# Other places in the planned order of two attentions: longer listed tasks of TensorE and other numbers for the kinds of tasks

## The chip, the cores and the metric

The kernel runs on one core of a Trainium2 chip, as one program. The metric is the device time of one execution in microseconds (us). A core has five engines that run side by side and wait for one another by semaphores: TensorE (PE, matrix products; its weight loads are shown as PEld), VectorE (DVE), ScalarE (ACT), GpSimd (POOL), and SyncE (SP), which here issues the transfers (DMAs). Each engine takes its instructions in the order in which the program lists them. PE writes its results to PSUM, eight banks of 512 fp32 columns on 128 partitions; the other data lie in SBUF.

## The reference

A decoder trunk of two layers on 1024 tokens of width 1024, with 16 heads of 64, all in fp32. What matters here are the two token mixers; each is followed by a gated MLP with a causal convolution.

```python
# layer 0: forgetting attention, per block of 128 queries
s = einsum('bhqd,bhkd->bhqk', qb, k) * scale
s = s + cb[..., :, None] - c[..., None, :]        # c: cumulated log of the forget gates
s = where(kpos <= qpos, s, -inf)
o = einsum('bhqk,bhkd->bqhd', softmax(s), v)
h = h + o @ w_out
...
# layer 1: sparse attention, two groups of 8 heads that share keys and values
p_c = softmax over 63 compressed keys;  o_c = p_c @ vc
o_s = softmax(q k_sel) @ v_sel   # 16 of 16 blocks of 64 tokens are chosen: causal attention
o_w = softmax(q k_win) @ v_win   # a window of 512 tokens
o = g0 * o_c + g1 * o_s + g2 * o_w
h = h + o @ w_out
```

## The kernel before, in words

An fp32 product is made from three matmuls: an operand is split into a high part (the value rounded to fp32r) and a low part (the rest), and high x high, high x low and low x high are added up in PSUM (lines 216 to 218, `mm3`). So most results pass ACT, which writes the high part, and then DVE or POOL, which writes the low part.

The stages follow each other: projections of the first attention; the forgetting attention; the rest of its output projection; the first MLP; projections of the second attention; the sparse attention; the second MLP.

**The planner.** In both attentions the order of instructions on each engine isn't written by hand: `Flow` (lines 103 to 175) holds a list of tasks, each with an engine, an estimated duration, a place and the buffers that it takes and gives back, and plays them through in time when the program is made. At each step it looks, on each engine, for the tasks that can start earliest, takes the one with the smallest place among them, and emits its instructions. The chip then runs each engine's list in that order. A task's place is `u` plus the number of its kind in `PLAN`; `gap` is added to the listed duration of PE's tasks alone:

```python
t = Task(eng, dur + (self.plan.get("gap", 0) if eng == "PE" else 0), u + self.plan.get(kind, 0), ...)
...
first = min(at for at, _ in c)
at, _, t = min(((at, t.prio, t) for at, t in c if at <= first), key=lambda x: x[1])
```

**Kinds in both attentions**, for a block of four times 128 queries of one head (first attention) or of 128 queries and four heads (second):
- R: PE makes scores into one of two score rooms of two PSUM banks (`scores`, line 585; the mask by line 590). M: DVE takes the maximum (lines 594, 599). E: ACT takes the exponential and its sum (line 602). D: DVE takes the reciprocal (line 605). N: POOL scales the probabilities (line 606).
- K, at u + 1 + x, with x from 0 to `spread` over the key blocks: PE turns up to four blocks of 128 x 128 into one of three banks `t` (line 619). H: ACT writes the high part (line 630). L: DVE the low part (line 632), into one of five or four buffers. V: PE adds the value product into the bank `v`, of which there is one (lines 624 and 625; a step is K, H, L, V in turn).
- J: ACT and DVE take the finished sum out of the bank `v` and join its halves (lines 644 and 648). O: in the sparse attention, POOL splits the joined rows.
- F and G: the first and the other seven steps of a half row of the output projection on PE, into a bank `t` (`proj_tasks`, line 835; F also turns rows for the next stage's norm). W: ACT and POOL split projection weights (`split_tasks`, lines 865 and 866). Q: everything else, all transfers on SP among it.

**The forgetting attention** (`fox_attn`, line 745). u counts 32 blocks: the first 24 are, for each of heads 0 to 7, its first and second half of queries and the first half of head h + 8; the last eight are the second halves of heads 8 to 15. A block in the first half has 4 blocks of keys, one in the second half 8. Beside them the planner lists the **late projections** (`late_tasks`, line 660): values, queries and keys of heads 8 to 15 for the second half of the tokens, 12 rows of eight steps (P is the first step of a row, S the others and the turn), row n at place `late` + 1.6 n with `late` = 2. A step is three matmuls of 512 columns, listed as .665 us plus `gap`. A row holds one of the three banks `t`. Rows of queries and keys then pass a norm of each head (`heads`, line 696: lines 708, 704, 249, 241, 242, 245 to 248, 707) and are stored to HBM (line 727), from where heads 8 to 15 load them (line 765). Loads of a head go out on SP in the order of u. The output projection of five row tiles can start when all 24 first blocks are joined. Probabilities have two buffers for each row of a block.

**The sparse attention** (`nsa_attn`, line 1960). Tiles of 128 queries go from the last to the first, i = 7 to 0, so with 1024 down to 128 keys. Each has two groups; a group has the compressed keys first (`cmp_tasks`, u grows by .5) and then four blocks (two quads of heads, each with all keys and with the window; u grows by 1 each). A tile's output projection (F, G) follows its joins. At the start three late rows of queries are projected (P) and normed (L246 to L248, L1519), and the output weights are split after them (W, place 2 + 3 k).

Of the kernel before, what the change touches and what calls it, by code (L numbers as in the profile page):

```python
# [16 lines left out]
P = 128  # L17
T = 1024
D = 1024
NT = T // P  # L20
ND = D // P
H = 16
HD = 64
G = 2
# [26 lines left out]
def moved(*shape):  # L51
# [2 lines left out]


PLAN = {
    "fox": dict(F=1e3, G=-11.5, R=.5, M=5, E=-1, K=-.5, H=-1.5, L=-5.5, V=2, J=-4, D=1.5, N=18.5, Q=1.5, W=13, P=-3, S=0, O=1, spread=.7, wo=.6, wo_from=21, side=2, late=2, step=1.6, gap=.015),
    "ffn0": {"": 18.5, "A": -1.5, "B": -11, "C": -11, "D": -10, "I": 4.5, "P": -12, "R": 14.5, "S": -6, "T": 23, "U": 24, "V": 23, "W": -7, "a": -2.5, "b": -12, "c": 12, "d": -7, "e": -12, "f": -4, "g": -20, "h": -8, "l": 21, "n": 16.5, "r": -8, "s": -6, "t": -6, "x": 23.5, "y": 23.5},
    "ffn1": {"": 0, "A": 12.5, "B": -4, "C": -12, "D": 12.5, "I": 15.5, "P": -11.5, "R": 3.5, "S": 12, "T": 18, "U": 24, "V": 17, "W": 4.5, "a": -12, "b": 8, "c": -12, "d": -3, "f": 0.5, "l": 19.5, "n": -11, "s": 17.5, "t": -8},
    "nin": {"": 0},  # L60
    "nsa": dict(P=5.5, S=-6, F=18, G=1e3, R=-6.5, M=11.5, E=.5, D=-5.5, K=-6, H=1, L=-2.5, V=9.5, J=13.5, O=24, N=0, Q=10, W=13, spread=.3, wo=3, wo_from=2, side=2, cmp=.5, gap=.02),
}


# [2256 lines left out]
```

## Time and profile before

| | |
|---|---|
| median of 3 runs | 2687.89 us (2687.56 to 2690.54) |
| the profiled execution: its own time | 2689.46 us |
| its span, first to last instruction | 2687.7 us |
| mean granted TensorE clock | 0.996 of full speed |
| forgetting attention | some 255 to 620 us of the span |
| sparse attention | some 1483 to 2045 us |

Times within the trace are us from the start of the span. Busy time of an engine is the union of its instructions; a matmul's end is modelled, since matmuls overlap, so that the start-to-start distance is the measure of its cost. Idle time before an instruction is shown in brackets with the releaser, the instruction that ended the last wait.

### The profile page before, as it was taken

How to read it: one execution, taken by the hardware profiler on the slowest of the kernel's cores; microseconds unless marked ns; L12 is line 12 of the kernel's file. 1: busy time of each engine (PE TensorE's matmuls, PEld its weight loads, DVE VectorE, ACT ScalarE, POOL GpSimd, SP SyncE). 2: the span in 40 equal slices, each digit the busy share in tenths (PEclk: the TensorE clock that was granted, in tenths of full speed). 3: DMA queues.
4: the chain of work that ended last, by engine and by line, in shares of the span. 5: the costliest groups of instructions: out<-in, count | busy, mean ns of one | idle time of the engine just before them, and what ended most of it. 6: DMA issues, size and time to landing. Idle time of an engine off the chain costs nothing.

```text
span 2687.7 us, 39265 instructions
## 1 busy us (share of the span) xinstructions
PE 2623.3 (98%) x13384; PEld 2178.8 (81%) x13384; DVE 2153.0 (80%) x4015; ACT 1509.1 (56%) x3168; POOL 550.4 (20%) x843
## 2 busy tenths in 40 slices
PE   8999999999999999999999999999999999999999
PEld 6778887787888888888898788888887788888887
DVE  6752778766987877889887888888987988777988
ACT  5331767655554545444674687777876555554443
POOL 1110444420000000000354564444452000000000
PEclk9999999999999999999999999999999999999999
DMA  6475666724422222734234310001123422224553
GB/s 183 107 170 174 178 164 179 203 64 152 127 87 94 71 94 86 272 120 157 100 97 123 94 60 13 33 29 36 41 68 120 136 96 77 93 72 168 188 173 129
DMA packets 276776, 310.84 MB, mean 116 GB/s; under 512 B 19944, under 2 KB 194448, under 8 KB 276576
## 3 DMA queue, kind: packets, MB, share of 16 engines
q1 hardware_dynamic: 276144, 306.76, 37.2%
q8 instruction: 106, 1.74, 0.3%
q10 hardware_dynamic: 432, 1.57, 0.2%
q14 instruction: 94, 0.77, 0.1%
HBM read 236.84 MB, written 71.43 MB: 115 GB/s over the span
## 4 chain that ended last, share of the span: by engine, by line
PE 63%; DVE 8%; ACT 2%; issue 1%; DMA 1%; POOL 0%; SPq 0%; DVEq 0%; ACTq 0%; POOLq 0%
PE ps L217 15%; PE ps L218 15%; PE ps L216 15%; PE t L619 4%; PE v L624 2%; PE s L1992 2%; PE v L625 2%; PE s L1991 2%; DVE op L1069 1%; PE t L216 1%; DVE sum L1069 1%; PE t L218 1%; PE t L217 1%; PE s L590 1%; DVE b L1069 1%
## 5 line engine op out<-in xcount | busy, mean ns | idle before, releaser
L1073 ACT CAST op<-sum 128x512 fp32r<-128x512 f32 x396 | 239.3, 621 | 401.5 <-PE ps L218 278.1
L216 PE MATMUL ps<-xs,op 128*128 128x512 f32 x880 | 342.6, 389 | 1.8 <-DVE u L1069 1.8
L217 PE MATMUL ps<-xs,op 128*128 128x512 f32 x880 | 342.5, 389 | 0.7 <-DVE xs L1069 0.7
L218 PE MATMUL ps<-xs,op 128*128 128x512 f32 x880 | 342.4, 389 | 0.0
L1069 DVE TENSOR_TENSOR op<-sum,op 128x512 fp32r<-128x512 f32 x396 | 266.9, 689 | 83.5 <-ACT op L1073 83.2
L602 ACT ACTIVATE pt<-s,sm 128x640 f32<-128x640 f32 (+7 forms) x384 | 275.0, 721 | 74.9 <-DVE sm L599 32.9
L632 DVE TENSOR_TENSOR p_l<-t,p_h 128x512 fp32r<-128x512 f32 x456 | 277.0, 628 | 47.5 <-ACT p_h L630 43.9
L630 ACT CAST p_h<-t 128x512 fp32r<-128x512 f32 x456 | 238.3, 545 | 112.9 <-PE t L619 109.4
L619 PE MATMUL t<-ident,pt 128*128 128x128 f32 x1632 | 242.7, 276 | 14.0 <-DVE p_l L632 6.9
L217 PE MATMUL ps<-op 128*128 128x512 f32 x616 | 239.9, 389 | 1.8 <-DVE op L1069 1.8
L216 PE MATMUL ps<-op 128*128 128x512 f32 x616 | 240.2, 390 | 0.4 <-ACT op L1073 0.4
L218 PE MATMUL ps<-op 128*128 128x512 f32 x616 | 239.7, 389 | 0.0
L606 POOL TENSOR_SCALAR pt<-pt,sm,gate 128x640 f32<-128x640 f32 (+7 forms) x256 | 199.3, 784 | 163.3 <-DVE sm L605 141.3
L599 DVE TENSOR_REDUCE sm<-s 128x1 f32<-128x640 f32 (+7 forms) x256 | 210.6, 833 | 24.9 <-PE s L590 20.4
L619 PEld LDWEIGHTS t<-ident,pt 128*128 128x128 f32 x1632 | 192.2, 142 | 46.8 <-DVE p_l L632 7.8
L1282 DVE SCALAR_TENSOR_TENSOR acc<-u,cw,acc 128x1023 f32<-128x1023 f32 (+1 forms) x176 | 225.7, 1283 | 4.1 <-ACT acc L1283 1.3
L216 PEld LDWEIGHTS ps<-xs,op 128*128 128x128 f32 x880 | 165.2, 188 | 37.2 <-issue 2.0
L217 PEld LDWEIGHTS ps<-xs,op 128*128 128x128 f32 x880 | 165.2, 188 | 35.1 <-DVE xs L1069 1.0
L218 PEld LDWEIGHTS ps<-xs,op 128*128 128x128 f32 x880 | 165.2, 188 | 34.3
L624 PE MATMUL v<-p_h,v 128*128 128x512 f32 (+1 forms) x376 | 157.9, 421 | 4.8 <-DVE o_early L648 2.5
L1073 ACT CAST op<-w_raw 128x512 fp32r<-128x512 f32 x132 | 81.5, 626 | 109.2 <-PE ps L218 103.9
L2216 POOL TENSOR_SCALAR h<-h,nt_rs 128x1024 f32<-128x1024 f32 x8 | 10.4, 1299 | 631.1 <-DVE nt_rs L248 612.4
(503 smaller groups left out, 6505.0 us busy)
## 6 DMA issues: line engine op xcount, KB each, us to landing
w_raw<-in_f_w_up SPq DMA_DIRECT2D x96, 512.0 KB
u<-in_f_w_down SPq DMA_DIRECT2D x176, 256.0 KB
s_g<-acc SPq DMA_DIRECT2D x40, 512.0 KB
g<-s_g SPq DMA_DIRECT2D x20, 1024.0 KB
w_raw<-in_a_w_in SPq DMA_DIRECT2D x32, 512.0 KB
qa<-s_q SPq DMA_DIRECT2D x32, 256.0 KB
ka<-s_k SPq DMA_DIRECT2D x32, 256.0 KB
v<-s_v SPq DMA_DIRECT2D x16, 512.0 KB
```

Of the source, the lines that this page charges most:

```text
L216: mm(out, a[0], b[0], start=start, stop=False, **kw)
L217: mm(out, a[0], b[1], start=False, stop=False, **kw)
L218: mm(out, a[1], b[0], start=False, stop=stop, **kw)
L599: b = a if joint else F.add("DVE", .066 + 1.0417e-3 * n, u, "M", lambda z=z, c=c: nc.vector.tensor_reduce(sm["nm"][:, c], src(ps.t, z), ax ...
L602: e = F.add("ACT", .238 + .8333e-3 * n, u, "E", lambda z=z, c=c, out=out: nc.scalar.activation(out(), src(ps.t, z), AF.Exp, bias=sm["nm"][ ...
L619: nc.tensor.transpose(t.t[:, r * P:(r + 1) * P], b(), self.ident)
L624: nc.tensor.matmul(out, v(), p2.t[0][:, :n], start=first, stop=False)
L630: h = F.add("ACT", .052 + .8333e-3 * n, u + 1 + x, "H", lambda: nc.scalar.copy(p2.t[0][:, :n], t.t[:, :n]), after=[a], uses=[t, p2])
L632: lambda: nc.vector.tensor_tensor(p2.t[1][:, :n], t.t[:, :n], f32(p2.t[0][:, :n]), op=OP.subtract), after=[h], uses=[t, p2])
L1069: TT = lambda out, a, b, op: nc.vector.tensor_tensor(out, a, b, op=op)
L1073: a = F.add("ACT", .53, u, "A", lambda: nc.scalar.copy(op.t[:, 0], src()), after, [op], uses)
L1282: return lambda: nc.vector.scalar_tensor_tensor(acc.t[:, sh:], o.t[:, :T - sh], cw[j][:, c:c + 1], acc.t[:, sh:], op0=OP.mult, op1=OP.add)
```

## The change

Only numbers of two plans change; the other plans, tasks, buffers and instructions are as before. The listed PE tasks are longer by .035 us (forgetting attention) and .03 us (sparse attention), and the kinds have other numbers.

```diff
-    "fox": dict(F=1e3, G=-11.5, R=.5, M=5, E=-1, K=-.5, H=-1.5, L=-5.5, V=2, J=-4, D=1.5, N=18.5, Q=1.5, W=13, P=-3, S=0, O=1, spread=.7, wo=.6, wo_from=21, side=2, late=2, step=1.6, gap=.015),
+    "fox": dict(F=1000.0, G=-8, R=-1.5, M=9.5, E=1.0, K=-2.0, H=-0.5, L=-12, V=0.5, J=0.5, D=9.5, N=22.5, Q=-11.0, W=3.5, P=-1.0, S=1.0, O=1, spread=0.7, wo=0.6, wo_from=21, side=2, late=2, step=1.6, gap=0.05),
...
-    "nsa": dict(P=5.5, S=-6, F=18, G=1e3, R=-6.5, M=11.5, E=.5, D=-5.5, K=-6, H=1, L=-2.5, V=9.5, J=13.5, O=24, N=0, Q=10, W=13, spread=.3, wo=3, wo_from=2, side=2, cmp=.5, gap=.02),
+    "nsa": dict(P=20.5, S=5.0, F=23.5, G=1000.0, R=4.5, M=12.0, E=20.0, D=-12, K=1.5, H=12.0, L=-10.0, V=20.0, J=14.0, O=22, N=19.0, Q=9.5, W=16.0, spread=0.3, wo=3, wo_from=2, side=2, cmp=0.5, gap=0.05),
```

## Rows read from the trace of the kernel before

**Rows 1.** The page's first part: each engine's busy time (share of the span) and its instructions.

```profile
PE 2623.3 (98%) x13384; PEld 2178.8 (81%) x13384; DVE 2153.0 (80%) x4015; ACT 1509.1 (56%) x3168; POOL 550.4 (20%) x843
```

**Rows 2.** Busy time by stage: the stretch in us from the span's start (the forgetting attention, then the sparse one), its length, each engine's busy us and instructions, the granted TensorE clock (1.00 is full), the DMA engines' busy share and GB/s.

```profile
255.00:620.00 365.00, 350.45 (x2029) 290.44 (x2028) 262.27 (x565) 238.54 (x560) 135.53 (x160) 0.99 0.57 161
...
1483.00:2045.00 562.00, 548.11 (x3520) 462.38 (x3520) 478.10 (x1016) 405.25 (x979) 279.69 (x378) 1.00 0.15 50
```

**Rows 3.** The same view, the forgetting attention cut finer; columns as in rows 2.

```profile
360.00:380.00 20.00, 18.01 (x111) 14.96 (x110) 17.10 (x42) 14.31 (x38) 5.86 (x8) 1.00 0.82 200
380.00:440.00 60.00, 59.48 (x354) 49.42 (x354) 47.53 (x115) 41.42 (x106) 24.36 (x32) 1.00 0.58 158
440.00:496.00 56.00, 46.17 (x270) 37.99 (x269) 43.39 (x95) 44.66 (x107) 37.44 (x40) 0.91 0.82 229
496.00:620.00 124.00, 123.75 (x693) 103.14 (x692) 80.58 (x141) 68.40 (x137) 26.84 (x27) 1.00 0.42 121
```

**Rows 4.** Two of these cuts with the instructions of line 217 alone, the second of each three matmuls of a projection step (up to 496 only late steps run it; columns: stretch, length, PE and weight loads, clock, DMA).

```profile
380.00:440.00 60.00, 12.55 (x32) 6.07 (x32) 1.00 0.58 158
440.00:496.00 56.00, 0.00 (x0) 0.00 (x0) 0.91 0.82 229
```

**Rows 5.** PE's waits from 436 to 496: who waited for whom, us in total, times, longest us.

```profile
PE t L619 <- DVE p_l L632: 4.0, 2, 2.2
PE v L624 <- DVE o_early L648: 2.5, 2, 1.5
PE v L624 <- DVE o_late L648: 2.0, 3, 0.8
```

**Rows 6.** Busy time in two short stretches between 440 and 496; columns as in rows 2.

```profile
448.80:455.60 6.80, 6.25 (x27) 5.97 (x28) 4.55 (x13) 4.49 (x11) 3.98 (x6) 0.50 0.85 261
...
486.30:489.70 3.40, 3.40 (x11) 2.69 (x12) 2.84 (x6) 2.40 (x7) 2.88 (x3) 0.50 0.81 255
```

**Rows 7.** Busy time in the sparse attention; columns as in rows 2.

```profile
1483.00:1530.00 47.00, 43.61 (x246) 34.06 (x246) 38.88 (x73) 29.39 (x60) 26.96 (x42) 0.96 0.33 92
...
1600.00:1900.00 300.00, 299.83 (x1946) 255.95 (x1945) 260.79 (x514) 216.79 (x485) 136.23 (x166) 1.00 0.08 26
1900.00:1960.00 60.00, 55.29 (x369) 45.96 (x367) 54.78 (x142) 48.83 (x143) 30.46 (x49) 1.00 0.18 62
```

**Rows 8.** PE in order of time (start us, us, instruction, xcount of like ones in a row): the first mask product of the blocks with u = 20 and with u = 25, which closes their first scores.

```profile
441.67 0.29 PE L590 MATMUL s<-mask_d,identb 128*128 128x128 bf16 x2
...
491.03 0.23 PE L590 MATMUL s<-mask_d,identb 128*128 128x128 bf16 x1
```

**Rows 9.** The timeline of all engines near 375, with the idle time before an instruction and what ended it: DVE's short operations of a late head's norm chain, POOL beside them, and PE.

```profile
374.85 0.17 DVE L246 TENSOR_TENSOR rs_t<-rs_t,rs_v 128x8 f32<-128x8 f32 x1
...
375.05 0.59 DVE L247 TENSOR_SCALAR rs_t<-rs_t 128x8 f32<-128x8 f32 x1
...
375.58 2.48 POOL L866 TENSOR_TENSOR w_l<-w_raw,w_h 128x512 fp32r<-128x512 f32 x2
375.67 1.19 DVE L248 TENSOR_TENSOR rs_r<-rs_y,rs_t 128x8 f32<-128x8 f32 x1
...
377.64 0.44 PE L619 MATMUL t<-ident,pt 128*128 128x128 f32 x2 [1.83 <-DVE w_raw L707]
```

**Rows 10.** The last late row and the first head that needs it: the row's last matmul, SP's issue of the last stores of its keys and of the first load of late keys (SPq is SP's own queue), and the first scores of that head.

```profile
438.86 0.39 PE L218 MATMUL t<-wo_h,wo_l 128*128 128x512 f32 x1
...
452.37 2.56 SPq L727 DMA_DIRECT2D s_k<-ohl_l  x2
...
458.14 1.11 SPq L765 DMA_DIRECT2D ka<-s_k  x2
...
473.22 0.40 PE L791 MATMUL s<-ka,qa 128*128 128x512 f32 x1
```

**Rows 11.** The timeline of all engines near 1517 in the sparse attention: POOL, DVE, and PE's wait.

```profile
1516.22 3.74 POOL L866 TENSOR_TENSOR wo_l<-w_raw,wo_h 128x512 fp32r<-128x512 f32 x3 [0.53 <-ACT wo_h L865]
1516.23 1.31 DVE L246 TENSOR_TENSOR w_raw<-w_raw 128x8 f32<-128x8 f32 x1
...
1520.76 0.48 PE L619 MATMUL t<-ident,pt 128*128 128x128 f32 x1 [3.15 <-DVE w_raw L1519]
```

**Rows 12.** PE at the first late steps: the first and the fourth of a row of matmuls of 512 columns.

```profile
255.09 0.39 PE L216 MATMUL t<-w_h,wo_h 128*128 128x512 f32 x1
...
255.77 0.39 PE L216 MATMUL t<-w_h,wo_h 128*128 128x512 f32 x1
```

**Rows 13.** Instructions from 1900 to 1962, in the sparse attention, by line and shape: line, engine, operation, out<-in, xcount | busy us, mean ns | idle us before, by releaser.

```profile
L602 ACT ACTIVATION_READ_ACCUMULATOR pt<-s,sm 128x1 f32 x38 | 7.9, 209 | 0.0
L606 POOL TENSOR_SCALAR pt<-pt,sm,gate 128x256 f32<-128x256 f32 x14 | 7.6, 554 | 5.7 <-DVE sm L605 4.1 <-PE s L1992 1.6
...
L602 ACT ACTIVATE pt<-s,sm 128x256 f32<-128x256 f32 x14 | 6.6, 486 | 0.5 <-DVE sm L594 0.5
...
L594 DVE TENSOR_REDUCE sm<-s 128x2 f32<-128x512 f32 x8 | 5.4, 681 | 0.0
```

**Rows 14.** PE: a turn of four blocks, and the instruction that follows the value product after it.

```profile
1939.84 0.61 PE L619 MATMUL t<-ident,pt 128*128 128x128 f32 x4
...
1940.75 0.49 PE L1014 MATMUL t<-ident,w_raw 128*128 128x128 f32 x3
```

**Rows 15.** PE's waits from 1900 to 1962, columns as in rows 5.

```profile
PE s L1991 <- ACT pt L602: 1.6, 2, 1.2
```

## The prediction

> **What bounds the kernel now.** I read the page's engine line first: TensorE (PE) is busy 98% of the span, the next engine, VectorE (DVE), 80% [rows 1]. So only PE's idle time, and time in which it runs slowly, can be won. Then busy time by stage [rows 2]: the plans that change order the two attentions alone, and there PE is idle 365.00 - 350.45 = 14.55 us and 562.00 - 548.11 = 13.89 us. Then each attention cut finer. In the forgetting attention [rows 3] 9.83 us of the idle time lie in one stretch, 440 to 496, and 360 to 380 has 1.99 us; from 496 to 620 PE is full. Counting the late projection's matmuls in the same cuts shows why [rows 4]: 32 of one line from 380 to 440, none from 440 to 496. They are filler: they need nothing from a softmax, and once they are used up PE waits for the softmax and for joins [rows 5]. The stretch also costs clock: from 448.8 to 455.6 and from 486.3 to 489.7 the granted clock is 0.50, that is 1.2 instead of 2.4 GHz [rows 6], after a wait of PE in each case. Half of 6.8 + 3.4 us is 5.1 us lost. So the stretch holds 9.83 + 5.1 = 14.9 us.
>
> In the sparse attention [rows 7] the idle time lies mainly at the start (3.39 us to 1530) and near the end (4.71 us from 1900 to 1960); the 300 us from 1600 are full, with DVE busy 87%.
>
> **The change, part by part.** No instruction is added or removed; the planner only lists them in another order on each engine. A kind's number is added to a task's place u (one u per head and half, or per head quad and branch), and the smallest sum goes first among tasks that can start at once.
>
> *Filler of the forgetting attention.* The late steps (S) go from 0 to +1, scores (R) from .5 to -1.5, turns (K) from -.5 to -2, value products (V) from 2 to .5. The last late row has place 2 + 11 x 1.6 = 19.6. Before, it ties with R of u = 19.1; after, 20.6 = u - 1.5 gives 22.1, so 3.0 u later. Against turns (u + 1 + x + K) and against V it is 2.5 u later. The starved stretch runs from the scores of u 20 to those of u 25 [rows 8], 49.3 us or 9.9 us per u, and is 56/9.9 = 5.7 u long. Filler that reaches 2.5 to 3.0 u further covers 0.44 to 0.53 of it. Of 14.9 us I take 0.5: **-7.5 us**. Bounds: 0 if buffers and data fix the order anyway, -14.9 if all is covered. Output steps (G, -11.5 to -8) cost nothing: they start only after the last first-half join, near 496, and there PE is full [rows 3].
>
> *Late heads' norm chain and weight splits* (Q 1.5 to -11, W 13 to 3.5). From 360 to 380, 1.83 us are a wait for a bank that such a chain frees [rows 9]. Q first on ScalarE (ACT) and DVE should end that wait, but the rows show that its length is that of L247 and L248, 0.59 and 1.19 us where the short form takes 0.17 (L246), while GpSimd (POOL) runs a weight split of 2.48 us. The Trainium skill (page SBUF — State Buffer, section "Who interferes with whom") says that a DVE instruction with two SBUF inputs and a GpSimd instruction that reads SBUF exclude each other for a whole instruction; the trace agrees in length, and by it Q gains nothing here while W comes earlier on POOL. From the rows: (0.59 - 0.17) + (1.19 - 0.17) = 1.44 of the 1.83 us stay, so **-0.4 us**, bounds -1.8 and +1.4 (one more such collision). POOL's scalings (N 18.5 to 22.5) already stood behind splits and stand there still. All loads carry Q, so their order among themselves in SP's queue stays.
>
> *What filler later makes late.* The last late row's matmuls end at 438.86, the last of its keys are sent until 454.93, and the first load of a head that needs them goes at 458.14, 15.1 us ahead of that head's scores at 473.22 [rows 10]. Filler 2.5 u (25 us) later, with 7.5 us won, puts the row's end near 456 and the send near 472, with the chain as long as now. The load then comes when its scores would be due (466); u 22 and 23 still have turns and values for about 20 us. SP issues in order: a key load that waits holds the query and value loads behind it. **+1 us**, bounds 0 and +10.
>
> *Maximum, reciprocal, join on DVE* (M +4.5, D +8, J +4.5, L -6.5): L was ahead of M already within the two-u lookahead that two probability buffers allow, so that pair keeps its order. Joins now stand behind every L. A join frees the only value bank; PE's waits for it are 2.5 + 2.0 us [rows 5], all where no filler is left. One L more ahead costs 0.6 us on DVE; with filler beside it, 0. Taken as 0, bound +4.5 (doubled).
>
> *Sparse attention.* Scores go from before to behind the turns of the u ahead of them (R - K from -.5 to +3), exps go last on ACT (E .5 to 20, casts H 1 to 12), filler stays last (G 1000; P 5.5 to 20.5, F 18 to 23.5). At the start the 3.15 us wait is the same collision, L246 at 1.31 us beside POOL's 3.74 us of splits, three of some 1.25 [rows 11]; late product, norm and split still follow each other, and on POOL the splits now come ahead of the scaling of probabilities (N 0 to 19, W 13 to 16). **0**, bounds -3.2 and +3. The 300 us between are full: **0**, bound +6. Near the end, **-1 us** of 4.71: reciprocals first and R later shift these waits rather than remove them; bounds -4.7 and the slow rival below.
>
> *Longer PE tasks* (gap .015 and .02 to .05). A step of three 512-column matmuls takes 3 x 0.227 = 0.681 us [rows 12]; planned it was .665 + .015, now .715. The planner sees less idle PE to fill, so it takes filler later, which helps the first part; on the chip PE reaches each result some 5% early. Worst, PE keeps the planned pace: 656 tasks (96 scores, 192 turns, 192 products, 96 late and 80 output steps, by the loops) x .035 = 23 us and about 880 x .03 = 26 us, the far bound. At best 0. DVE at 72% in one and 85% in the other [rows 2] can keep up, so near the lower end: **+0.5 us**.
>
> Sum: -7.5 - 0.4 + 1 - 1 + 0.5 = -7.4. The profiled execution took 2689.46 us (its span 2687.7 and 1.8 around it), 1.57 above the median of 2687.89. 2689.46 - 7.4 = 2682.1, and at the median's level **2680.5 us**. About 0.2%, 5.4 us, is what a measurement of this kernel can tell from no change.
>
> **Rivals.**
> *Buffers hold, not order.* PE's waits in the starved stretch end with a join, that is the one value bank, or with a split of turns that frees a turn bank [rows 5]. If banks decide, the same waits return beside any order: about 2686, within the bound. Against it: from 380 to 440 the same banks with filler leave PE 0.52 us idle in 60 [rows 3]. The Trainium skill (page Perfetto Trace Analysis, section "Optimization Strategy") says that consistent gaps on the engine that should be full can mean too little PSUM for the next tile. By that rule the time would stay; the trace speaks against it by the stretch just named.
> *The listed order hardly moves* because only tasks startable at the same moment are compared: 2688. The numbers move by more than the lookahead of about two u for S and E, which speaks against it.
> *Exps last starve the small tiles: slower.* With 256 keys a pair's chain is 0.68 (maximum) + 0.49 + 0.21 (exp) + 0.55 (scaling on POOL) = 1.9 us and a reciprocal [rows 13], the cover by turns and values 2 x 0.91 = 1.8 us (one of each takes 1940.75 - 1939.84 [rows 14]). Where the chain is the longer one, at 256 keys and fewer, scores that no longer run ahead leave PE waiting in each of 16 u. At the longest wait of this sort now, 1.2 us [rows 15], that is 19 us: 2680.5 + 19 = 2699.5. For it: that wait exists. Against: buffers let scores run whenever no turn is ready.
> *Both gaps close.* The whole 14.9, 3.2, 4.7 and 1.8 us: 2687.9 - 24.6 = 2663.3.
>
> **Chances.** Forecast (5.4 to 16 us faster) .38, both gaps .12, buffers or an unmoved order .24, slower by the exps .26. So faster .50, same .24, slower .26. The range leaves out the far part of the closing of both gaps and of the slow rival, a tenth each: 2663 to 2701. The forecast's own range is 2672 to 2683.
>
> **What would show it.** Right: late matmuls (one line) after 440, fewer idle us and no half clock from 440 to 500, the sparse middle still full. Wrong: key loads of the late heads going out after their scores' time, PE waits for exps after 1900, DVE's short operations at 1.2 us beside splits more often than now, or PE waiting in the 300 us that are full today.

## The result, and the profile after

The changed kernel takes 2707.09 us, median of 6 runs (2702.53 to 2711.51); the kernel before, on the same chip, 2689.12 (2687.56 to 2691.27). The ratio is 1.0067, 95% interval 1.0057 to 1.0077: 18.0 us slower, where 7.4 us faster had been forecast, and above the range. The profiled execution took 2702.53 us, span 2700.7, the shortest of the six, 13.1 us more than the profiled one before. Times and ratios leave out two slow executions, one of 2919 us of the run with PE's kinds alone and one of 7889 us of the kernel before beside it.

Two rows of TensorE (PE) for each kernel give the length of the forgetting attention with the rest of its projection, from the first late step (at 255.09 before, [rows 12]) to the first turn of the first MLP. The kernel before, then the kernel after (start us, us, instruction, idle before it):

```profile
673.96 1.93 PE L1154 MATMUL ps<-ident,h_rows 128*128 128x128 f32 x8 [2.25 <-POOL h_rows L1143]
```

```profile
253.31 0.39 PE L216 MATMUL t<-w_h,wo_h 128*128 128x512 f32 x1
...
689.90 1.97 PE L1154 MATMUL ps<-ident,h_rows 128*128 128x128 f32 x8 [2.15 <-POOL h_rows L1143]
```

418.9 us became 436.6: +17.7. The sparse attention gives back 1.7 (first score to last output step, 556.3 to 554.6 us); so the stage of the forgetting attention holds the whole loss. (It began 1.8 us earlier in this execution, and 1.1 us less lie elsewhere: 17.7 - 1.7 - 1.8 - 1.1 = 13.1.)

Next, where in it. Busy time by stretch: length, then busy us of PE, weight loads, DVE, ACT, POOL, the granted clock, the DMA engines' busy share, GB/s. First the kernel before in stretches that were not shown ahead of the prediction:

```profile
255.00:450.00 195.00, 187.04 (x1110) 154.23 (x1109) 148.01 (x351) 134.14 (x340) 76.81 (x99) 1.00 0.60 169
450.00:520.00 70.00, 63.65 (x373) 53.13 (x372) 52.75 (x110) 52.26 (x119) 40.19 (x43) 0.94 0.85 222
520.00:620.00 100.00, 99.75 (x551) 83.08 (x550) 61.50 (x106) 52.14 (x103) 18.53 (x20) 1.00 0.33 102
620.00:700.00 80.00, 75.89 (x355) 61.84 (x354) 64.91 (x129) 46.37 (x112) 5.25 (x4) 0.98 0.41 129
```

The kernel after, in the same stretches and then in two of [rows 3]:

```profile
255.00:450.00 195.00, 190.90 (x1133) 155.32 (x1132) 146.87 (x354) 133.22 (x341) 76.47 (x100) 1.00 0.58 167
450.00:520.00 70.00, 55.14 (x274) 43.58 (x272) 43.72 (x86) 43.46 (x98) 37.27 (x37) 0.85 0.77 201
520.00:620.00 100.00, 98.89 (x563) 83.03 (x564) 66.74 (x120) 57.20 (x115) 22.36 (x23) 1.00 0.30 90
620.00:700.00 80.00, 72.42 (x337) 59.20 (x336) 52.55 (x110) 41.78 (x104) 6.33 (x4) 0.96 0.44 143
...
360.00:380.00 20.00, 20.00 (x121) 16.52 (x120) 16.91 (x43) 14.53 (x40) 7.39 (x11) 1.00 0.50 141
440.00:496.00 56.00, 45.52 (x247) 36.27 (x245) 40.84 (x89) 40.37 (x96) 29.04 (x31) 0.91 0.65 182
```

PE's idle time, length less busy: up to 450 it fell from 7.96 to 4.10 us; from 450 to 520 it rose from 6.35 to 14.86; from 520 to 620 from 0.25 to 1.11; from 620 to 700 from 4.11 to 7.58. That is -3.9 + 8.5 + 0.9 + 3.5 = +9.0. The rest is clock. Before, 13.6 us ran at 0.50 [rows 6, and 3.4 us from 674.0]; after, these five stretches:

```profile
457.60:461.10 3.50, 3.50 (x19) 3.21 (x16) 3.25 (x6) 2.39 (x6) 1.17 (x2) 0.51 0.59 185
481.60:488.40 6.80, 6.78 (x24) 5.91 (x25) 2.67 (x5) 3.28 (x8) 3.93 (x4) 0.50 0.77 180
498.70:508.90 10.20, 7.86 (x25) 6.28 (x26) 4.85 (x8) 6.34 (x11) 8.31 (x7) 0.50 1.08 230
648.80:652.20 3.40, 3.40 (x10) 2.66 (x9) 1.89 (x3) 2.49 (x7) 0.00 (x0) 0.51 0.47 154
689.80:693.20 3.40, 3.30 (x12) 3.01 (x13) 3.37 (x6) 2.15 (x9) 0.05 (x1) 0.50 0.44 128
```

They are 27.3 us, 13.7 more, and half of that, 6.8 us, is lost. With 9.0 this makes 15.8 of the 17.7; the rest was not followed further. So the filler did what it should up to 450 us, and the starved stretch was not filled. It moved some 9 to 12 us further: PE's waits in it run from 454.1 to 501.0, where they ran from 442.0 to 492.1, so it is nearly as long as before, and poorer. Few late steps got there: the instructions of line 217 in the stretches of [rows 4] are 30 and 7, where they were 32 and 0:

```profile
380.00:440.00 60.00, 11.69 (x30) 5.69 (x30) 1.00 0.62 165
440.00:496.00 56.00, 2.74 (x7) 1.14 (x6) 0.91 0.65 182
```

Now what PE waits for there (us in total, times, longest), to be read beside [rows 5]; first the stretch from 436 to 520, then from 620 to 700:

```profile
PE s L791 <- ACT pt L602: 5.8, 5, 3.9
PE t L619 <- DVE p_l L632: 2.8, 2, 1.7
PE t L714 <- DVE w_raw L707: 2.6, 1, 2.6
PE s L791 <- DMA ka<-s_k: 2.3, 1, 2.3
...
PE ps_t L965 <- POOL h_rows L961: 5.4, 2, 3.8
```

The waits for a turn bank and for joins shrank (4.0 + 2.5 + 2.0 before). In their place stand exps, a late norm chain (2.6 us, 1.2 before), late keys, and at the stage's end a norm. The timeline shows each (SPq is SP's own queue):

```profile
453.45 2.49 POOL L866 TENSOR_TENSOR wo_l<-w_raw,wo_h 128x512 fp32r<-128x512 f32 x2
...
453.53 1.22 DVE L247 TENSOR_SCALAR rs_t<-rs_t 128x8 f32<-128x8 f32 x1
454.78 1.18 DVE L248 TENSOR_TENSOR rs_r<-rs_y,rs_t 128x8 f32<-128x8 f32 x1
...
456.74 0.66 PE L714 MATMUL t<-ident,w_raw 128*128 128x128 f32 x4 [2.60 <-DVE w_raw L707]
...
468.53 1.26 SPq L727 DMA_DIRECT2D s_k<-ohl_l  x2
...
471.11 1.12 SPq L765 DMA_DIRECT2D ka<-s_k  x2
...
480.98 0.49 PE L791 MATMUL s<-ka,qa 128*128 128x512 f32 x1 [2.33 <-DMA ka<-s_k]
...
491.64 0.53 SPq L900 DMA_DIRECT2D w_raw<-in_a_w_out  x1
...
498.96 1.14 ACT L865 CAST wo_h<-w_raw 128x512 fp32r<-128x512 f32 x2 [3.07 <-DMA w_raw<-in_a_w_out]
...
500.00 0.89 ACT L602 ACTIVATE pt<-s,sm 128x768 f32<-128x768 f32 x1
...
501.04 0.80 PE L791 MATMUL s<-ka,qa 128*128 128x512 f32 x1 [3.95 <-ACT pt L602]
...
631.80 0.33 SPq L936 DMA_DIRECT2D h_rows<-s_h  x1
633.21 0.33 SPq L946 DMA_DIRECT2D h_rows<-in_x  x1
633.76 0.33 SPq L859 DMA_DIRECT2D s_h<-w_raw  x1
639.87 0.33 SPq L979 DMA_DIRECT2D h_rows<-s_h  x1
...
647.47 1.09 PE L965 MATMUL ps_t<-ident,h_rows 128*128 128x128 f32 x8 [3.82 <-POOL h_rows L961]
```

At 453 the collision of [rows 9] has come back, now in the last late row. The last late matmul ends its row at 450.15 (438.86 before, [rows 10]), its keys go out until 469.8 and not 454.9, the first load of late keys goes at 471.11 and not 458.14, and the scores at 480.98 wait for it. At 498.96 ACT stands 3.07 us for the load of an output weight, with an exp queued behind the cast and PE behind the exp. At the end the last row's store (L859) goes behind two loads of 512 KB, and the load that reads it back (L979) follows 6.1 us later; before it followed 2.6 us later, with no such load just ahead of the store:

```profile
622.21 0.32 SPq L859 DMA_DIRECT2D s_h<-w_raw  x1
...
624.83 0.32 SPq L979 DMA_DIRECT2D h_rows<-s_h  x1
```

### The profile page after: what moved, and what is told of

It reads as the page before. It is cut to its first block, busy times and chain, and to the rows that moved or that the text cites. A ratio compares the mean times of both kernels' runs of the same rounds, so it can differ in the third digit from the quotient of the medians.

```text
span 2700.7 us, 39262 instructions
## 1 busy us (share of the span) xinstructions
PE 2633.8 (98%) x13384; PEld 2179.7 (81%) x13384; DVE 2147.7 (80%) x4015; ACT 1510.9 (56%) x3168; POOL 554.0 (21%) x843
## 4 chain that ended last, share of the span: by engine, by line
PE 63%; DVE 8%; ACT 2%; issue 2%; DMA 1%; POOL 0%; SPq 0%; DVEq 0%; ACTq 0%; POOLq 0%
PE ps L217 15%; PE ps L216 15%; PE ps L218 15%; PE t L619 4%; PE s L1991 2%; PE v L624 2%; PE s L1992 2%; PE v L625 2%; DVE op L1069 1%; DVE sum L1069 1%; PE t L216 1%; PE t L218 1%; PE t L217 1%; PE s L590 1%; PE v L2067 0%
## 5 line engine op out<-in xcount | busy, mean ns | idle before, releaser
L606 POOL TENSOR_SCALAR pt<-pt,sm 128x896 f32<-128x896 f32 (+6 forms) x128 | 96.2, 758 | 224.6 <-DVE sm L605 155.1
```

The costliest lines, as they stand in the source:

```text
L606: ("POOL", (.327 if gate else .24) + .8333e-3 * n, "N", lambda r=r, c=c, out=out: nc.gpsimd.tensor_scalar(out(), out(), sm["rs"][:, c], ga ...
```

## The experiments

All runs are given against the kernel before on the same chip, as a ratio with its 95% interval. A diff shows the numbers of the first attention's plan ("fox") that change; "from before" or "from after" names the kernel that is edited.

**Where the loss is, and two suspects.** Theory A: filler that goes later makes late data late. Theory B: the loss comes from the longer listed tasks, that is from PE's list being planned too slowly.

From before, with the whole new plan of the first attention and the old one of the second (e1_fox_only):

> The changed plan of the forgetting attention alone, the sparse attention's as before. By the traces of before and after, the forgetting attention and the way out of it (first late step to the first turn of the first MLP) grew from 418.9 to 436.6 us, 17.7 us, and the sparse attention (its first score to its last output step) went from 556.3 to 554.6 us. All theories that put the loss into the first attention expect some 2707 us, 1.007 of before. A theory that splits the loss between both expects some 2698.

2708.53, ratio 1.0079 (1.0064 to 1.0094). The first attention holds all of it. Its counterpart, the new plan of the second attention alone:

```diff
-    "nsa": dict(P=5.5, S=-6, F=18, ... gap=.02),
+    "nsa": dict(P=20.5, S=5.0, F=23.5, ... gap=0.05),
```

> The kernel before with the second attention's new plan alone. The stage took 1.7 us less in the kernel after, so the theory that nothing passes between the stages says 2687.4 (ratio 0.9994), too little for the measurement to tell from no change; over 2692, or under 2684, would say that the two plans are not independent.

2689.32, ratio 1.0000 (0.9991 to 1.0009): nothing that can be measured, and the two plans are independent as far as these runs tell. The stage of the forgetting attention is 440.7 us long in the trace of the first run and 422.3 in that of the second, 18.4 apart again; against 436.6 and 418.9 above, it also shows that a stage read from one execution is good to some 4 us.

From after, the weight casts put back (W; e2_split_back), since the ACT wait at 498.96 stands on one:

```diff
- W=3.5
+ W=13
```

> The change with W of the forgetting attention back at 13: weight casts stand behind the exps on ScalarE again. Theory 'cast in front' (after: ScalarE waits 3.07 us for a weight load with an exp behind it, PE then idles 3.95 us, and the half clock from 498.7 to 508.9 follows): that stall and its 10.2 us of half clock go, 3.95 + 5.1 = 9 us less, some 2698 us. Theory 'filler too late' (late rows' keys reach HBM 15 us later, heads 8 and on wait): the cast is one of several waits beside it; 2704 us or more, and another stall stands in the same place.

2708.93, ratio 1.0074 (1.0058 to 1.0091): no change. W isn't what puts that cast ahead of the exp; it still stands there, the load it waits for is as late, and PE waits 3.10 us at 501.20:

```profile
499.12 1.14 ACT L865 CAST wo_h<-w_raw 128x512 fp32r<-128x512 f32 x2 [2.25 <-DMA w_raw<-in_a_w_out]
```

So what that wait costs was not found out.

From after, late steps earlier than even before (e3_filler_back), and the listed length put back (e4_gap_back):

```diff
- P=-1.0, S=1.0
+ P=-5, S=-2
```

> The change with P = -5 and S = -2 in the forgetting attention, so that late steps again stand half a place ahead of scores, as before the change. Theory 'filler too late': late matmuls end near 435 instead of 447, the last late keys are stored some 12 us sooner, the wait of PE for a key load (2.3 us) is gone, and two thirds of the loss return: 2695 us or less. Theory 'cast in front': no more than 3 us return, 2704 us.

```diff
- gap=0.05
+ gap=.015
```

> The change with the listed length of PE's tasks in the forgetting attention back at .015. Theory 'pace' (the planner takes PE for slower than it is and lists results too early): most of the 18 us return, 2693 us or less. Theories 'filler too late' and 'cast in front' rest on the kinds' numbers: within 4 us of the changed kernel, 2703 to 2711 us.

2696.75, ratio 1.0035 (1.0022 to 1.0048), and 2693.80, ratio 1.0023 (1.0013 to 1.0034). Either brings back more than half of the 18 us, so neither is the cause by itself. Both traces also lack the late store at the stage's end: it goes 7.7 us or more behind the last load and is read back 2.6 us later. With the listed length put back PE is idle 0.3 us from 620 to 700, at full clock, where the kernel after has 7.6 us and 6.8 us at half clock. So a large part of what comes back lies at the end of the stage, not in the starved stretch.

**One part alone, from before.** The listed length (e5_gap_alone), PE's kinds F, G, R, K, V, P, S (e6_pe_kinds_alone), the kinds of all other engines (e7_other_kinds_alone), late steps alone (e9_filler_alone), in this order:

```diff
- gap=.015
+ gap=.05
```

> Before, with the listed length of PE's tasks in the forgetting attention at .05 and nothing else. Taking the length back cost the changed kernel 13 us. Theory 'pace' (a PE listed 5% too slow gives an order in which PE meets its waits, whatever the kinds' numbers): 8 to 13 us slower than before, 2697 to 2702, with more waits of PE all over the stage. Theory 'the two make each other worse' (length and numbers both push the late steps back, each alone little): within 5 us of before.

```diff
- G=-11.5, R=.5, K=-.5, V=2, P=-3, S=0
+ G=-8, R=-1.5, K=-2.0, V=0.5, P=-1.0, S=1.0
```

> Before, with the new numbers of the forgetting attention's PE kinds alone (F, G, R, K, V, P, S). Theory 'filler too late': this holds the whole shift of the late steps by 2.5 to 3 places; late keys are stored 10 us or more later than before, 8 us slower or more, 2697 or more. Theory 'pace' and theory 'engines in between': within 5 us of before.

```diff
- M=5, E=-1, H=-1.5, L=-5.5, J=-4, D=1.5, N=18.5, Q=1.5, W=13
+ M=9.5, E=1.0, H=-0.5, L=-12, J=0.5, D=9.5, N=22.5, Q=-11.0, W=3.5
```

> Before, with the new numbers of the kinds on ScalarE, VectorE and GpSimd alone (M, E, D, H, L, J, N, Q, W). Theory 'engines in between' (casts and late norms in front of exps, joins and reciprocals behind turns): 8 us slower or more with waits of PE for exps. Theory 'filler too late' and theory 'pace': within 5 us of before, 2684 to 2694.

```diff
- P=-3, S=0
+ P=-.5, S=2.5
```

> Before, with P and S of the forgetting attention 2.5 higher and nothing else, the smallest form of the shift. Theory 'filler too late': late matmuls end some 10 us later than before, the last late keys too, and the kernel is slower by 5 us or more, 2694 or more. The forecast of the prediction (filler that lasts longer covers the starved stretch): 5 to 8 us faster, 2681 to 2684.

| part alone | us | ratio | over before |
|---|---|---|---|
| listed length | 2693.33 | 1.0014 (1.0004 to 1.0024) | +4 |
| PE's kinds | 2697.07 | 1.0028 (1.0016 to 1.0041) | +8 |
| other engines' kinds | 2689.63 | 1.0003 (0.9994 to 1.0013) | 0 |
| late steps 2.5 u later | 2693.78 | 1.0015 (1.0006 to 1.0025) | +5 |

The last row tests the step of the prediction that carried its sum, and it has the wrong sign: -7.5 expected, +4.7 measured. The time alone doesn't say why: a move of a tenth of that size costs as much (further down, "Place or chance?"). The trace says more. These are the run's stretches, then two of PE's waits from 436 to 520:

```profile
255.00:450.00 195.00, 190.26 (x1127) 155.97 (x1126) 145.83 (x354) 134.57 (x339) 76.32 (x100) 0.99 0.59 168
450.00:520.00 70.00, 58.99 (x317) 47.62 (x316) 47.78 (x96) 48.76 (x111) 38.27 (x39) 0.90 0.76 207
...
PE s L791 <- DMA ka<-s_k: 2.1, 1, 2.1
...
PE s L792 <- DMA kb<-s_k: 1.1, 1, 1.1
```

Idle time up to 450 falls by 3.2 us, from 450 to 520 it rises by 4.7, and PE waits 3.2 us for late keys, which it does neither in the kernel before nor in the small move. So the late steps' number by itself makes the pattern of the whole change in small. The first three rows add up to 12 or 13 us, not to 18 (the last is a piece of PE's kinds).

**Do length and PE's kinds feed each other?** Both together, from before (e12_gap_and_pe_kinds):

> The kernel before with the gap of .05 and with the kinds of PE (F, G, R, K, V, P, S) of the first attention's new plan; the kinds of the other engines and all of the second attention as before. Alone, gap gave +4, PE's kinds +8, the other kinds 0. If gap and PE's kinds add up: about 2701. If they feed each other (both put filler later, and the later it is the more each us costs): 2704 to 2709, as the whole plan. If the other kinds are needed for the loss: under 2699.

2696.18, ratio 1.0025 (1.0014 to 1.0037). Less than the sum and no more than PE's kinds alone, so they don't; the third forecast, that the other kinds are needed, holds by its number. Yet those alone are worth 0. The parts don't add up.

**The mirror image.** Late steps 2.5 u earlier, from before (e11_filler_earlier):

```diff
- P=-3, S=0
+ P=-5.5, S=-2.5
```

> The kernel before with late steps placed 2.5 u earlier alone (P -5.5, S -2.5): the mirror image of the run with filler later alone, which gave 2693.8. Theory A: late keys come earlier, they bind nowhere in the kernel before, so nothing is won; filler is used up 25 us sooner and the starved stretch grows by that much at its rate of loss (14.9 us in 56): 2691 to 2696. Rival: the starved stretch has a fixed length set by the exps and joins, it only moves: 2687 to 2691. Theory B says nothing.

2701.38, ratio 1.0048 (1.0030 to 1.0066): worse than 2.5 u later, and above both forecasts. In its profile the time goes ahead of 450, where PE is busy 181.22 us of 195 at a mean clock of 0.96 (187.04 at 1.00 before). So the old place lies between two losses.

**Late data taken away.** The second halves of heads 8 to 15 read other heads' data, from after (e10_no_late_data) and, as its control, from before (e13_before_no_late_data); then the same data with the kernel after's lists on PE, DVE, ACT and POOL kept (e14_order_kept), so that only SP's transfers no longer wait (the lines of the loads, which then take `src_h`, `p_in` and `a_in`, are left out of the diff):

```diff
- q_there, k_there, v_there = stored if h >= half and g else ([], [], [])
+ q_there, k_there, v_there = [], [], []        # e14: as before
+ src_h = h - half if h >= half and g else h    # source of the loads
+ p_in, a_in = divmod(src_h, 2)
```

> The kernel after, but the second halves of heads 8 to 15 load queries, keys and values of heads 0 to 7, which lie in HBM from the start, so no head needs the late projections any more; these are still computed and stored (the output of heads 8 to 15 is thus another one). The planner knows of no wait for late rows either. Theory A (the filler that goes later makes late keys late, and the waits behind them are the loss): the loss goes, 2686 to 2695 us. Theory B (the loss is in the first part, where the plan packs PE's list too slowly, and keys are only one of its marks): it stays, 2702 to 2709. Between them: a share of each, read from the time of the first late scores and from the waits of PE.

> The kernel before, with the second halves of heads 8 to 15 reading queries, keys and values of heads 0 to 7 (other output), as in the run of the kernel after that came back to 2689.6 us: the control of that run. Theory A (late data bind after the change and not before it): no change, 2686 to 2692. Rival C (late data bind in both, and taking them away is worth some 17 us in any plan): 2669 to 2676.

> The kernel after, reading early heads' data as before in that run, but with the planner still told that late rows must be there: PE, DVE, ACT and POOL keep the lists of the kernel after to the last instruction, only transfers on SP no longer wait for late data. If PE waits on the chip for data that are late: near the run without late data, 2686 to 2695. If the loss is in the order that the planner lists because it believes them late: it stays, 2702 to 2709.

| | us | ratio |
|---|---|---|
| after, no late data | 2689.59 | 1.0005 (0.9996 to 1.0014) |
| before, no late data | 2687.44 | 0.9990 (0.9981 to 0.9998) |
| after's lists, data not late | 2698.99 | 1.0032 (1.0020 to 1.0044) |

Without late data the new plan costs nothing that can be measured, and the old one gains 1.8 us. But both lists are planned anew, so this alone doesn't show that the whole loss needs the late data. With the lists kept, half comes back (1.0067 to 1.0032, some 9 us, 5 to 14 by the two intervals): that much comes from PE waiting on the chip for data that are late. The time lies between the two forecasts for this run, so both missed. In its waits from 450 to 520 the keys' line is gone:

```profile
PE s L791 <- ACT pt L602: 6.2, 6, 2.9
PE t L714 <- DVE w_raw L707: 2.6, 1, 2.6
PE t L619 <- DVE p_l L632: 2.1, 2, 1.1
PE t L619 <- DVE w_raw L855: 1.3, 1, 1.3
PE v L624 <- DVE o_late L648: 0.6, 1, 0.6
```

That line was only 2.3 us; the rest came behind it: the first output step is 243.3 us after the stage's start, 251.1 in the kernel after. (Behind it 2.5 us are lost again, so the two traces differ by 5.3 us in this stage; the profiled execution of the kernel after is its shortest.) Of the other half, the wait at the stage's end is one part. Here are 450 to 520 and 620 to 700 of the run with lists kept, then of the run from after without late data:

```profile
450.00:520.00 70.00, 57.07 (x305) 45.46 (x304) 48.55 (x95) 48.16 (x108) 39.25 (x40) 0.90 0.77 202
...
620.00:700.00 80.00, 72.68 (x332) 59.44 (x331) 55.40 (x113) 41.12 (x103) 5.26 (x4) 0.94 0.38 120
```

```profile
450.00:520.00 70.00, 54.76 (x308) 45.24 (x307) 48.98 (x97) 49.19 (x110) 40.18 (x40) 0.88 0.75 213
...
620.00:700.00 80.00, 78.52 (x376) 64.27 (x374) 59.81 (x115) 43.48 (x105) 6.15 (x4) 1.00 0.41 132
```

With the lists kept, 7.3 us are idle after 620 (4.1 before), at a clock of 0.94. In the other run, whose list was planned anew, only 1.5 us are idle there at full clock, while from 450 to 520 PE is as idle as in the kernel after (15.2 and 14.9 us). So that run wins its time in the last stretch and in clock (17.1 us at half speed, not 27.3) and not by filling the starved one: it is no proof that late keys alone cost 18 us. The run with lists kept is the clean one, and it says 9.

The traces split in two at the stage's end. In the kernel after and in the five runs with its plan of this attention or one next to it (that plan alone, W put back, lists kept, the small move below, G put back; 2699 us or more) the last row's store goes 0.6 us behind a load of 512 KB and is read back 6.1 to 6.7 us later. In the kernel before and the other thirteen runs, the two without late data among them, the nearest load is 7.7 us or more ahead and the store is read back after 2.6 us. So the run from after without late data differs from the one with lists kept in this order too, and part of what it wins lies there.

**Place or chance?** Small moves of both plans, from after (e15_after_nudged) and from before (e16_before_nudged):

```diff
- P=-1.0, S=1.0, gap=0.05
+ P=-0.8, S=1.2, gap=0.045
...
- P=-3, S=0, gap=.015
+ P=-2.8, S=.2, gap=.02
```

> The kernel after with the first attention's P, S and gap moved a little (+.2, +.2, -.005). If its loss has a cause that goes with the filler's place: 2702 to 2709 again. If such loss is luck of one order, which any small move deals anew: anywhere from 2689 to 2709, and the more it moves the less the single plan says.

> The kernel before with the same small moves (P and S +.2, gap +.005). If the place of the filler sets the time smoothly: 2687 to 2691, no change. If any reshuffled order costs: 2692 to 2700, and then the kernel before is one lucky order rather than a good place of the filler.

2703.69, ratio 1.0047 (1.0033 to 1.0061), and 2693.56, ratio 1.0015 (1.0004 to 1.0027). From before, moves of a tenth to a fifth of the change already cost 4 us: the kernel before is one good order, not a broad place. So the 4 and 5 us of the listed length and of the late steps alone can't be told, by time, from what a new order of PE can cost at this spot. From after, 14.5 of the 18.0 us stay (12.6 by the ratio), so its loss isn't that of one order only; but a single neighbour was run.

**The other half.** From after, the output steps' number put back (e17_output_back), and late steps and listed length put back together (e18_filler_and_gap_back):

```diff
- G=-8
+ G=-11.5
```

> The kernel after with the number of the first attention's output steps alone put back (G -8 to -11.5). In the kernel after PE loses 11.0 us between the last output step and the first MLP, 4.6 more than before, with a wait of 3.8 for the norm of the row that the last output steps make. If G's new number leaves those steps for the end: that part comes back, 2701 to 2704. If they are late because all before them is late: no change, 2705 to 2709.

```diff
- P=-1.0, S=1.0, gap=0.05
+ P=-3, S=0, gap=.015
```

> The kernel after with the places of the late steps and the listed length both put back in the first attention (P -3, S 0, gap .015). If late data, made late by these two, are the whole cause: 2687 to 2691. If the other numbers of PE's kinds (G, R, K, V) carry a part of their own: 2692 to 2698; gap put back alone gave 2693.8.

2707.92, ratio 1.0071 (1.0057 to 1.0085): the wait at the end isn't G's doing. And 2713.13, ratio 1.0090 (1.0076 to 1.0105): the slowest of all, with both suspects at their old values. Its stretches show that its loss is in part another one: 16.0 us idle ahead of 450 (4.1 in the kernel after), the starved stretch as idle as there or more (17.0 us, 14.9 in the kernel after), and nothing at the end:

```profile
255.00:450.00 195.00, 178.97 (x1039) 145.64 (x1039) 134.44 (x327) 124.28 (x316) 71.13 (x93) 0.99 0.55 155
450.00:520.00 70.00, 52.99 (x284) 43.36 (x283) 42.86 (x97) 44.70 (x105) 36.90 (x39) 0.80 0.72 204
...
620.00:700.00 80.00, 79.62 (x384) 64.93 (x383) 50.79 (x104) 41.06 (x103) 5.23 (x4) 1.00 0.44 148
```

With this, theory A in its simple form (the late steps' number and the listed length make the loss) falls. It didn't take the lateness away, though: its scores, turns and values are still put ahead, 1.5 to 2 lower, against them the late steps are late again, and the last store of late keys is issued 217.3 us after the stage's start (215.8 in the kernel after, 198.3 before). Lateness is not enough either: with the listed length put back in the kernel after it is issued at 216.3, and the time is 2693.8.

**What is shown and what stays open.** Shown: the loss lies in the first attention; some 9 of 18 us come from waits on the chip for late data. Supported by a list planned anew, not isolated: without late data nothing of the loss is left. Read from the traces, not isolated: of the other 9, the store that lands behind two loads at the end, with its clock, is some 5 (3.5 us more idle time and half of 3.4 at half clock); no run changed that order by itself. Open: which numbers make which order. Each of the fourteen plans with other numbers or lengths for PE's tasks in this attention, the kernel after among them, was slower than before, by 4 to 25 us, as long as late data were used. No run with late data beat the kernel before by what can be measured.

## Why the prediction was wrong

- *What bounds the kernel*: right as a reading (idle time and half clock from 440 to 496), wrong as an offer. In both kernels the stretch starves from 3 to 4 us behind the last late matmul (438.86 and 442.0, 450.15 and 454.1).
- *Filler of the forgetting attention*, -7.5 us: **the step that failed**. It took the starved stretch for fixed in place and filler for free to move into it. But the filler makes the queries and keys of the very blocks that follow. Moved alone it costs +4.7 us where -7.5 was forecast, and PE then waits 3.2 us for late keys; the size of that loss is no more than a small move of the plan costs, the missing gain is plain. In the whole change idle time up to 450 did fall by 3.9 us, and from 440 to 496 there were 7 late steps; the stretch slid behind them, from 450 to 520 PE was 8.5 us more idle and twice as long at half clock. The bounds 0 and -14.9 left no room for a loss; only the next term had any.
- *What filler later makes late*, +1 us (0 to +10): the mechanism was named with its place (send near 472, load when scores are due at 466). The chip gave a send until 469.8, a load at 471.11 and scores at 480.98, so the send was right within 3 us, but the scores came 15 us later than forecast, and the size is some 9 us instead of 1, inside the bound of 10. The 20 us of turns and values that were to cover it did not cover it all: PE stood 2.33 us for those keys, and more behind them.
- *Late heads' norm chain and weight splits*, -0.4: the wait of [rows 9] went (360 to 380 is full, 20.00 us), and the same collision stands at 453 with 2.60 us, within the bound of +1.4 on balance. The cause given, after the Trainium skill (page SBUF — State Buffer, section "Who interferes with whom"), fits again: 1.22 and 1.18 us on DVE beside 2.49 on POOL. (L248 has the two SBUF inputs of that rule; L247, held as long, has one.) By kinds alone the run with the other engines' numbers gives 0.
- *Maximum, reciprocal, join*, 0: right, by the same run; PE's waits for joins even fell from 4.5 to 0.5 us.
- *Output steps* at nothing: G back alone changes nothing, but the cover named (PE full from 496) ended at 620, and the norm behind the last row was not looked at. There, behind the store that is read back late, 3.5 us of idle time appeared.
- *Longer PE tasks*, +0.5: alone +4.2, well inside the far bound of 23, and mis-sized, though no more than a small move costs. That its side effect, filler listed later, helps was not borne out: the late steps alone, moved later, don't.
- *Sparse attention*, -1: the stage is 1.7 us shorter, the run of it alone 0.7; neither can be told from no change.
- Of the rivals, the slower one (exps last in the sparse attention, 2699.5) came near the time by another mechanism in another stage: the sparse stage is not slower. That one did not hold. The rivals by which the time stays, or both gaps close, are out by the time. Adding the terms up as independent was a fault too: the parts measured alone give 12 or 13, together 18, with two put back 25.

## What to carry to other kernels

Before filler is moved into a hole, ask what waits for the filler's own results: here it fed the blocks behind the hole, and the hole moved with it. In a list planned by greedy choice one number also moves work far from where it is aimed (here the store at the stage's end), so terms of a sum don't add; run the number alone, its mirror image and a fraction of it before trusting a direction, and hold a loss against what the fraction costs. To price a dependence, take away the lateness of the data and keep every engine's list; a list planned anew wins or loses elsewhere too.

## What was not expected of the hardware

- Half clock (1.2 GHz): each of the five stretches begins in or just behind a wait of PE of 2.15 to 3.95 us, and together they are 27.3 us where 13.6 were: 6.8 of the 17.7 us. The longest, 10.2 us, begins in the wait of 3.95.
- A store of 512 KB behind two loads of 512 KB, issued 2.0 and 0.6 us ahead, was read back 6.1 us after its issue, and 6.1 to 6.7 us in all six traces with that order. In the fourteen others, with no load within 7.7 us ahead, it was 2.6 us.
